# Grouped instance norm on one core: 64 KB rows in three 8 MB slots, and an earlier gamma

## The chip, the cores and the metric

The kernel runs on one core of a Trainium2 chip. The metric is the device time of one execution in microseconds, and the median of several runs is what is compared. The core has a tensor engine (PE), a vector engine (DVE), a scalar engine (ACT), a general engine (POOL) and a queue engine (SP), and 16 DMA engines that carry data between HBM, where input and output lie, and SBUF, the on-chip memory of 128 partitions. Transfers are issued here from SP's queue and from ACT's queue, and both run on the same 16 DMA engines.

## The reference

The input `x` has 4 x 128 = 512 channels of 256 x 256 float32 values, 134.2 MB. Each channel is normalised by its own mean and variance and multiplied by one gamma per channel of the group layout:

```
mu = x.mean(axis=(3, 4), keepdims=True)
var = ((x - mu) ** 2).mean(axis=(3, 4), keepdims=True)
out = (x - mu) / np.sqrt(var + 1e-5) * gamma[None, :, :, None, None]
```

Every value is read once from HBM and written once, 268.4 MB in all, if a channel stays in SBUF from its load to its store.

## The kernel before

A channel's 65536 values are cut into 8 rows of 8192 values (32 KB), one row to a partition, so a unit of 128 partitions holds 16 channels and 4 MB. There are 32 units (`U`) and six slots in SBUF (`xt0` to `xt5`, line 45).

The program writes its order out by hand (line 43 switches automatic scheduling off), so each engine executes its instructions in the order of the source. Lines 51 to 55 issue the first six loads: units 1 and 3 from ACT's queue, the others from SP's queue, and the row of 128 gammas (`g_row`) from SP's queue after unit 0. POOL then makes small constants: `eps_t`, `one`, and `navg` (lines 62 to 71), a 128 x 128 matrix with -1/65536 where two partitions hold the same channel, and zero elsewhere.

The loop over units (lines 100 to 133) does the following for each unit.

- DVE sums each row (line 102), and ACT squares each row and sums the squares (line 103). The squares themselves go into `junk` and aren't used.
- In unit 0 only, `gamma_columns` (lines 77 to 89) follows on DVE and PE: it repeats each gamma over the partitions of its channel and turns the row into columns `g_col` with eight small matmuls.
- PE multiplies both row sums by `navg` (line 113). This gives every partition minus the mean and minus the mean square of its channel.
- DVE combines the two to minus the variance (line 114), ACT takes the root (line 118), DVE the reciprocal (line 122) and the product with gamma (line 124).
- DVE rewrites the slot in place: (x - mean) x scale (line 127).
- ACT's queue issues the store (line 131), and SP's queue the load of the unit six later into the same slot (line 133). That load waits until the store has landed.

A float32 matmul appears in the profile as two passes, each a weight load (PEld) and a product (PE).

Of the kernel before, what the change touches and what calls it, by code (L numbers as in the profile page):

```python
# [1 line left out]

# [4 lines left out]

F32 = mybir.dt.float32
U8 = mybir.dt.uint8
ALU = mybir.AluOpType  # L10
ACTF = mybir.ActivationFunctionType
AX = mybir.AxisListType


@with_exitstack
def kernel(
    ctx: ExitStack,
    tc: tile.TileContext,
    x: bass.AP,
    gamma: bass.AP,  # L20
    out: bass.AP,
):
    nc = tc.nc
    B, G, C, H, W = x.shape
    P = nc.NUM_PARTITIONS
    HW = H * W
    n_ch = B * G * C
    S = 8
    K = P // S
    F = HW // S  # L30
    U = n_ch // K
    NG = (G * C) // K
    AHEAD = 6
    assert HW % S == 0 and (G * C) % K == 0

    xv = x.rearrange("b g c h w -> (b g c h w)").rearrange("(u p f) -> u p f", p=P, f=F)
    ov = out.rearrange("b g c h w -> (b g c h w)").rearrange("(u p f) -> u p f", p=P, f=F)
    gv = gamma.rearrange("g c -> (g c)")

    data = ctx.enter_context(tc.tile_pool(name="data", bufs=1))  # L40
    singles = ctx.enter_context(tc.tile_pool(name="singles", bufs=1))
    psum = ctx.enter_context(tc.tile_pool(name="psum", bufs=4, space=bass.MemoryType.PSUM))
    ctx.enter_context(tc.manual_schedule())

    slots = [data.tile([P, F], F32, name=f"xt{i}") for i in range(AHEAD)]

    def load(u, queue):
        queue.dma_start(out=slots[u % AHEAD][:], in_=xv[u])  # L48


    g_row = singles.tile([1, G * C], F32, name="g_row")
    for u in range(AHEAD):
        load(u, nc.scalar if u in (1, 3) else nc.sync)
        if u == 1:
            nc.sync.dma_start(out=g_row[:], in_=gv[None, :])


    eps_t = singles.tile([P, 1], F32, name="eps_t")
    nc.gpsimd.memset(eps_t[:], 1e-5)  # L59
    one = singles.tile([1, 1], F32, name="one")  # L60
    nc.gpsimd.memset(one[:], 1.0)
    navg = singles.tile([P, K, S], F32, name="navg")
    nc.gpsimd.memset(navg[:], -1.0 / HW)  # L63
    nc.gpsimd.affine_select(  # L64
        out=navg[:], in_=navg[:], pattern=[[-S, K], [0, S]], compare_op=ALU.is_ge,
        fill=0.0, base=0, channel_multiplier=1,
    )
    nc.gpsimd.affine_select(  # L68
        out=navg[:], in_=navg[:], pattern=[[S, K], [0, S]], compare_op=ALU.is_ge,
        fill=0.0, base=S - 1, channel_multiplier=-1,  # L70
    )
    navg_w = navg[:].rearrange("p k s -> p (k s)")
    g_rep = singles.tile([1, NG, K, S], F32, name="g_rep")
    g_ps = psum.tile([P, NG], F32, name="g_ps", bufs=1)
    g_col = singles.tile([P, NG], F32, name="g_col")

    def gamma_columns():
        nc.vector.tensor_copy(  # L78
            out=g_rep[:],
            in_=g_row[:].rearrange("o (n k) -> o n k", n=NG).unsqueeze(3).to_broadcast([1, NG, K, S]),  # L80
        )
        for n in range(NG):
            nc.tensor.matmul(  # L83
                out=g_ps[:, n : n + 1],
                lhsT=g_rep[:, n].rearrange("o k s -> o (k s)"),
                rhs=one[:],
                start=True, stop=True,
            )
        nc.vector.tensor_copy(out=g_col[:], in_=g_ps[:])  # L89

    junk = singles.tile([P, F], U8, name="junk")

    st = singles.tile([P, U, 2], F32, name="st")
    nvar = singles.tile([P, U], F32, name="nvar")
    std = singles.tile([P, U], F32, name="std")
    rstd = singles.tile([P, U], F32, name="rstd")
    scale = singles.tile([P, U], F32, name="scale")

    squares = []
    for u in range(U):  # L100
        t = slots[u % AHEAD]
        nc.vector.reduce_sum(out=st[:, u, 0:1], in_=t[:], axis=AX.X)  # L102
        square = nc.scalar.activation(  # L103
            out=junk[:], in_=t[:], func=ACTF.Square, accum_out=st[:, u, 1:2],
        )
        if u:

            tc.declare_no_dep(square.ins, squares[-1].ins, reason="junk, ordered by the root between")
        squares.append(square)
        if u == 0:  # L110
            gamma_columns()
        ps = psum.tile([P, 2], F32, name="ps")
        nc.tensor.matmul(out=ps[:], lhsT=navg_w, rhs=st[:, u], start=True, stop=True)  # L113
        nc.vector.tensor_scalar(  # L114
            out=nvar[:, u : u + 1], in0=ps[:, 0:1], scalar1=ps[:, 0:1],
            scalar2=ps[:, 1:2], op0=ALU.mult, op1=ALU.add,
        )
        nc.scalar.activation(  # L118
            out=std[:, u : u + 1], in_=nvar[:, u : u + 1], func=ACTF.Sqrt,
            bias=eps_t[:], scale=-1.0,  # L120
        )
        nc.vector.reciprocal(out=rstd[:, u : u + 1], in_=std[:, u : u + 1])  # L122
        g = u % NG
        nc.vector.tensor_mul(  # L124
            out=scale[:, u : u + 1], in0=rstd[:, u : u + 1], in1=g_col[:, g : g + 1],
        )
        nc.vector.tensor_scalar(  # L127
            out=t[:], in0=t[:], scalar1=ps[:, 0:1], scalar2=scale[:, u : u + 1],
            op0=ALU.add, op1=ALU.mult,
        )  # L130
        nc.scalar.dma_start(out=ov[u], in_=t[:])
        if u + AHEAD < U:
            load(u + AHEAD, nc.sync)


# [1 line left out]
_INS = ['x', 'gamma']  # L137
_OUTS = [((4, 8, 16, 256, 256), 'float32')]


# [23 lines left out]
```

## Time and profile before

| What | Value |
|---|---|
| median of 8 runs | 627.08 us (626.85 to 627.22) |
| the profiled execution | 626.85 us, of which its span, first to last instruction, is 625.1 us |
| DVE busy | 442.9 us, 71% of the span |
| ACT busy | 239.9 us, 38% |
| PE busy | 21.4 us, 3% |
| HBM | 134.22 MB read, 134.22 MB written, 429 GB/s over the span |
| line 102, DVE row sum, 128 x 8192 | 32 times 8683 ns |
| line 103, ACT squares, 128 x 8192 | 32 times 7030 ns, each followed by 186 ns to read the sum |
| line 127, DVE write-back, 128 x 8192 | 32 times 4550 ns |
| lines 114, 118, 122, 124 (128 x 1) | 287, 294, 164 and 159 ns |
| ACT's table load | two, 1283 ns each |
| loads | 32 of 4 MB, median 29.0 us from issue to landing (30 on SP's queue) |
| stores | 32 of 4 MB, median 64.1 us from issue to landing |

The table is read from the profile's summary page and its groups of instructions. A time between issue and landing includes the time that a transfer waits behind others on its queue. The share of busy time of an engine is a mean over the whole span.

### The profile page before, as it was taken

The numbers are of one execution on the slowest core, as the hardware profiler recorded it, in microseconds if no ns is written. First come the engines' busy times: TensorE is split into PE (matmuls) and PEld (weight loads), VectorE is DVE, ScalarE is ACT, GpSimd is POOL, SyncE is SP. The second block draws the span as 40 slices with busy tenths as digits, with TensorE's granted clock in tenths as the row PEclk, the third lists the DMA queues.
The fourth block names the chain that finished last, engine by engine and source line by source line (L and its number), as shares of the span: only waits on it lengthen the run. The fifth ranks groups of instructions, "written<-read, shape, count | busy, mean of one in ns | idle before, by whom it ended". The sixth has DMA issues, their size and how long they took to land.

```text
span 625.1 us, 628 instructions
## 1 busy us (share of the span) xinstructions
PE 21.4 (3%) x80; PEld 19.5 (3%) x80; DVE 442.9 (71%) x162; ACT 239.9 (38%) x98; POOL 1.3 (0%) x9
## 2 busy tenths in 40 slices
PE   0020000000000000000000000000000000000000
PEld 0020000000000000000000000000000000000000
DVE  0569999999898767867668676686766877667710
ACT  0435555544444423444224442244432444323400
POOL 0000000000000000000000000000000000000000
DMA  8999999999999999999999999999999999999998
GB/s 369 436 436 419 419 436 436 436 436 436 435 436 435 426 428 434 428 436 436 434 436 436 434 436 432 426 432 430 432 436 434 436 436 432 436 436 430 428 434 359
DMA packets 9220, 268.46 MB, mean 429 GB/s; under 512 B 1025, under 2 KB 1026, under 8 KB 1026
## 3 DMA queue, kind: packets, MB, share of 16 engines
q10 hardware_dynamic: 4896, 142.61, 52.8%
q1 hardware_dynamic: 4322, 125.83, 46.8%
q14 instruction: 2, 0.02, 0.0%
HBM read 134.22 MB, written 134.22 MB: 429 GB/s over the span
## 4 chain that ended last, share of the span: by engine, by line
DMA 62%; DVE 30%; PE 2%; issue 1%; ACT 1%; SPq 0%; ACTq 0%
DMA xt<-in_x_dram 55%; DVE st L102 24%; DMA out_dram<-xt 7%; DVE xt L127 5%; PE ps L113 2%; DVE nvar L114 1%; PE g_ps L83 1%; ACT std L118 0%; ACT L118 0%; DVE rstd L122 0%; DVE scale L124 0%; DVE g_rep L78 0%; SPq L48 0%; ACTq L118 0%
## 5 line engine op out<-in xcount | busy, mean ns | idle before, releaser
L102 DVE TENSOR_REDUCE st<-xt 128x1 f32<-128x8192 f32 x32 | 277.9, 8683 | 110.2 <-DMA xt<-in_x_dram 110.2
L103 ACT ACTIVATE junk<-xt 128x8192 uint8<-128x8192 f32 x32 | 224.9, 7030 | 266.1 <-DMA xt<-in_x_dram 212.1
L127 DVE TENSOR_SCALAR xt<-xt,ps,scale 128x8192 f32<-128x8192 f32 x32 | 145.6, 4550 | 1.2
L118 ACT ACTIVATE std<-nvar,eps_t 128x1 f32<-128x1 f32 x32 | 9.4, 294 | 76.0 <-DVE nvar L114 76.0
L113 PE MATMUL ps<-st,navg 128*128 128x2 f32 x64 | 17.9, 349 | 536.4 <-DVE st L102 536.4
L113 PEld LDWEIGHTS ps<-st,navg 128*128 128x128 f32 x64 | 16.1, 312 | 538.2 <-issue 538.2
L114 DVE TENSOR_SCALAR nvar<-ps 128x1 f32<-128x1 f32 x32 | 9.2, 287 | 23.5 <-PE ps L113 23.5
L122 DVE RECIPROCAL rstd<-std 128x1 f32<-128x1 f32 x32 | 5.2, 164 | 12.9 <-ACT std L118 12.9
L103 ACT ACTIVATION_READ_ACCUMULATOR junk<-xt 128x1 f32 x32 | 6.0, 186 | 0.0
L124 DVE TENSOR_TENSOR scale<-rstd,g_col 128x1 f32<-128x1 f32 x32 | 5.1, 159 | 1.1
L83 PE MATMUL g_ps<-one,g_rep 1*128 1x1 f32 x16 | 3.5, 347 | 32.1 <-DVE g_rep L78 32.1
L83 PEld LDWEIGHTS g_ps<-one,g_rep 1*128 1x128 f32 x16 | 3.5, 325 | 32.0 <-issue 32.0
L118 ACT ACT_TABLE_LOAD x1 | 1.3, 1283 | 6.8 <-DVE nvar L114 6.8
L89 DVE COPY g_col<-g_ps 128x8 f32<-128x8 f32 x1 | 0.2, 165 | 3.7 <-PE g_ps L83 3.7
L103 ACT ACT_TABLE_LOAD x1 | 1.3, 1283 | 1.7 <-PEq L148 1.7
L78 DVE COPY g_rep<-g_row 1x1024 f32<-1x1024 f32 x1 | 0.7, 672 | 0.0
L64 POOL TENSOR_SCALAR_AFFINE_SELECT navg<-navg 128x128 f32<-128x128 f32 x1 | 0.4, 403 | 0.1
L68 POOL TENSOR_SCALAR_AFFINE_SELECT navg<-navg 128x128 f32<-128x128 f32 x1 | 0.4, 398 | 0.1
L63 POOL MEMSET navg<- 128x128 f32 x1 | 0.2, 221 | 0.0
L148 POOL MEMSET const-bfloat16-1.0<- 128x1 bf16 x1 | 0.1, 101 | 0.0
L148 POOL MEMSET const-uint8-127<- 128x1 uint8 x1 | 0.1, 101 | 0.0
L59 POOL MEMSET eps_t<- 128x1 f32 x1 | 0.1, 99 | 0.3 <-POOLq L148 0.3
(3 smaller groups left out, 0.3 us busy)
## 6 DMA issues: line engine op xcount, KB each, us to landing
out_dram<-xt ACTq DMA_DIRECT2D x32, 4096.0 KB, 64.1
xt<-in_x_dram SPq DMA_DIRECT2D x30, 4096.0 KB, 29.0
xt<-in_x_dram ACTq DMA_DIRECT2D x2, 4096.0 KB, 31.5
g_row<-in_gamma_dram SPq DMA_DIRECT2D x1, 0.5 KB
```

Source lines behind the costliest of these rows:

```text
L64: nc.gpsimd.affine_select(out=navg[:], in_=navg[:], pattern=[[-S, K], [0, S]], compare_op=ALU.is_ge, fill=0.0, base=0, channel_multiplier=1,)
L68: nc.gpsimd.affine_select(out=navg[:], in_=navg[:], pattern=[[S, K], [0, S]], compare_op=ALU.is_ge, fill=0.0, base=S - 1, channel_multipli ...
L78: nc.vector.tensor_copy(out=g_rep[:], in_=g_row[:].rearrange("o (n k) -> o n k", n=NG).unsqueeze(3).to_broadcast([1, NG, K, S]),)
L83: nc.tensor.matmul(out=g_ps[:, n : n + 1], lhsT=g_rep[:, n].rearrange("o k s -> o (k s)"), rhs=one[:], start=True, stop=True,)
L102: nc.vector.reduce_sum(out=st[:, u, 0:1], in_=t[:], axis=AX.X)
L103: square = nc.scalar.activation(out=junk[:], in_=t[:], func=ACTF.Square, accum_out=st[:, u, 1:2],)
L113: nc.tensor.matmul(out=ps[:], lhsT=navg_w, rhs=st[:, u], start=True, stop=True)
L114: nc.vector.tensor_scalar(out=nvar[:, u : u + 1], in0=ps[:, 0:1], scalar1=ps[:, 0:1], scalar2=ps[:, 1:2], op0=ALU.mult, op1=ALU.add,)
L118: nc.scalar.activation(out=std[:, u : u + 1], in_=nvar[:, u : u + 1], func=ACTF.Sqrt, bias=eps_t[:], scale=-1.0,)
L122: nc.vector.reciprocal(out=rstd[:, u : u + 1], in_=std[:, u : u + 1])
L124: nc.vector.tensor_mul(out=scale[:, u : u + 1], in0=rstd[:, u : u + 1], in1=g_col[:, g : g + 1],)
L127: nc.vector.tensor_scalar(out=t[:], in0=t[:], scalar1=ps[:, 0:1], scalar2=scale[:, u : u + 1], op0=ALU.add, op1=ALU.mult,)
```

## The change

The unit becomes twice as large. A channel is now 4 rows of 16384 values (64 KB), and a unit holds 32 channels and 8 MB; there are 16 units (`V`) and three slots. Each load and each store of a unit is issued as two transfers of 64 rows, 4 MB each: the first 16 channels of the unit go to the even partitions (`t[0::2]`), the others to the odd partitions (`t[1::2]`). All loads are issued from SP's queue, and a half's next load waits for the same half's store. `navg` gets more steps on POOL, because partitions of one channel now lie two apart.

The gamma row is the first transfer on ACT's queue. A root of `eps_t` on ACT, whose result isn't used, comes before the loop and brings the table load with it, and the gamma columns are made ahead of the loop as well.

Within a unit, the squares are taken in two halves of 8192 columns, three matmuls replace one, and the write-back is split by columns: DVE takes the first 10240 (subtract and multiply) and ACT the other 6144 (multiply and add `shift`, which is minus mean times scale).

Unit 13, the third last, is stored in four transfers with rows of 32 KB. For the last unit the statistic is shared: DVE runs `bn_stats` over 18 pieces of 512 columns, ACT squares and sums the other 7168, and the two parts are added by matmuls that accumulate in one PSUM tile; its write-back and its store go in two halves of columns.

The core of the diff, without the unchanged small steps:

```diff
-    S = 8
-    F = HW // S
-    U = n_ch // K
-    AHEAD = 6
+    SL = 3
+    FW = HW // 4
+    FN = FW // 2
+    V = n_ch // 32
+    DV = 10240
+    BN, BW = 18, 512
...
+    xw = xf.rearrange("(v h r f) -> v h r f", h=2, r=P // 2, f=FW)
+    ow = of.rearrange("(v h r f) -> v h r f", h=2, r=P // 2, f=FW)
...
-    g_row = singles.tile([1, G * C], F32, name="g_row")
-    for u in range(AHEAD):
-        load(u, nc.scalar if u in (1, 3) else nc.sync)
-        if u == 1:
-            nc.sync.dma_start(out=g_row[:], in_=gv[None, :])
+    def load_slot(v):
+        t = slots[v % SL]
+        for h in range(2):
+            nc.sync.dma_start(out=t[h::2], in_=xw[v, h])
+
+    g_row = singles.tile([1, GC], F32, name="g_row")
+    nc.scalar.dma_start(out=g_row[:], in_=gv[None, :])
+    for v in range(SL):
+        load_slot(v)
...
+    root_eps = singles.tile([P, 1], F32, name="root_eps")
+    nc.scalar.activation(out=root_eps[:], in_=eps_t[:], func=ACTF.Sqrt)
...
+    for d in (-6, -4, -2, 0, 2, 4, 6):
+        nc.gpsimd.affine_select(
+            out=navg[:], in_=navg[:], pattern=[[-8, P // 8], [-1, 8]],
+            compare_op=ALU.not_equal, fill=-1.0 / HW, base=-d, channel_multiplier=1,
+        )
...
+    navg_b = singles.tile([P, P], F32, name="navg_b")
+    nc.gpsimd.tensor_scalar(
+        out=navg_b[:], in0=navg_w, scalar1=float(BN * BW), scalar2=None, op0=ALU.mult,
+    )
...
+    def sums(v, t, ps):
+        nc.vector.reduce_sum(out=st[:, v, 0:1], in_=t[:], axis=AX.X)
+        squared(v, t, 0, FN, 1)
+        squared(v, t, FN, FW, 2)
+        nc.tensor.matmul(out=ps[:, 0:1], lhsT=navg_w, rhs=st[:, v, 0:1], start=True, stop=True)
+        nc.tensor.matmul(out=ps[:, 1:2], lhsT=navg_w, rhs=st[:, v, 1:2], start=True, stop=False)
+        nc.tensor.matmul(out=ps[:, 1:2], lhsT=navg_w, rhs=st[:, v, 2:3], start=False, stop=True)
+
+    def sums_shared(v, t, ps):
+        e = BN * BW
+        bs = singles.tile([P, BN, nc.vector.BN_STATS_DIM], F32, name="bs")
+        for k in range(BN):
+            nc.vector.bn_stats(out=bs[:, k], in_=t[:, k * BW : (k + 1) * BW])
+        squared(v, t, e, FW, 1)
+        squared(v, t, e, FW, 0, ACTF.Identity)
+        mv = singles.tile([P, nc.vector.BN_AGGR_DIM], F32, name="mv")
+        nc.vector.bn_aggr(out=mv[:], in_=bs[:])
...
+        nc.tensor.matmul(out=ps[:], lhsT=navg_b[:], rhs=me[:], start=True, stop=False)
+        nc.tensor.matmul(out=ps[:], lhsT=navg_w, rhs=st[:, v, 0:2], start=False, stop=True)
...
-        nc.vector.tensor_scalar(
-            out=t[:], in0=t[:], scalar1=ps[:, 0:1], scalar2=scale[:, u : u + 1],
-            op0=ALU.add, op1=ALU.mult,
-        )
-        nc.scalar.dma_start(out=ov[u], in_=t[:])
-        if u + AHEAD < U:
-            load(u + AHEAD, nc.sync)
+        nc.vector.tensor_mul(out=shift, in0=ps[:, 0:1], in1=scale)
+
+        parts = [(0, FW)] if v < V - 1 else [(0, FN), (FN, FW)]
+        for a, b in parts:
+            m = a + DV * (b - a) // FW
+            nc.scalar.activation(
+                out=t[:, m:b], in_=t[:, m:b], func=ACTF.Identity, bias=shift, scale=scale,
+            )
+            nc.vector.tensor_scalar(
+                out=t[:, a:m], in0=t[:, a:m], scalar1=ps[:, 0:1], scalar2=scale,
+                op0=ALU.add, op1=ALU.mult,
+            )
+
+
+            for c, d in [(a, b)] if v != V - SL else [(0, FN), (FN, FW)]:
+                for h in range(2):
+                    nc.scalar.dma_start(out=ow[v, h, :, c:d], in_=t[h::2, c:d])
+        if v + SL < V:
+            load_slot(v + SL)
```

## The prediction

> **What bounds the kernel now.** I read the page's queue table and slices first, then the chain of waits, then stretches of the span, then the last microseconds in order of time. The page says who is full:
>
> ```profile
> GB/s 369 436 436 419 419 436 436 436 436 436 435 436 435 426 428 434 428 436 436 434 436 436 434 436 432 426 432 430 432 436 434 436 436 432 436 436 430 428 434 359
> DMA packets 9220, 268.46 MB, mean 429 GB/s; under 512 B 1025, under 2 KB 1026, under 8 KB 1026
> ...
> q10 hardware_dynamic: 4896, 142.61, 52.8%
> q1 hardware_dynamic: 4322, 125.83, 46.8%
> ...
> DMA xt<-in_x_dram 55%; DVE st L102 24%; DMA out_dram<-xt 7%; DVE xt L127 5%; PE ps L113 2%; DVE nvar L114 1%; PE g_ps L83 1%; ACT std L118 0%; ACT L118 0%; DVE rstd L122 0%; DVE scale L124 0%; DVE g_rep L78 0%; SPq L48 0%; ACTq L118 0%
> ```
>
> The two queues' packets fill 52.8 + 46.8 = 99.6% of 16 engines' span: no engine slot is left for a hidden gap. The chain's 24% of DVE comes from units 0 to 5, where the chain walks through compute although loads and stores go on beside it. The answer by stretches shows that (span, then busy times, last column GB/s):
>
> ```profile
> 22.00:46.00 24.00, 4.06 (x18) 3.99 (x18) 17.51 (x8) 11.18 (x5) 0.00 (x0) 1.00 0.99 427
> ...
> 66.00:120.00 54.00, 2.24 (x8) 2.01 (x8) 49.29 (x21) 24.38 (x11) 0.00 (x0) 1.00 1.01 437
> 120.00:580.00 460.00, 13.96 (x50) 12.54 (x50) 343.42 (x125) 183.59 (x75) 0.00 (x0) 1.00 1.00 433
> ...
> 596.00:622.00 26.00, 0.00 (x0) 0.00 (x0) 0.00 (x0) 0.00 (x0) 0.00 (x0) 1.00 1.02 440
> 622.00:623.70 1.70, 0.00 (x0) 0.00 (x0) 0.00 (x0) 0.00 (x0) 0.00 (x0) 1.00 0.14 58
> 623.70:625.10 1.40, 0.00 (x0) 0.00 (x0) 0.00 (x0) 0.00 (x0) 0.00 (x0) 1.00 0.00 0
> ```
>
> The rate stays within 1.5% of its mean from 22 to 622 us, whatever the engines do. The rest is 1.8 us before the first data packet and 1.4 us after the last. The end, in order of time:
>
> ```profile
> 561.09 7.03 ACT L103 ACTIVATE junk<-xt 128x8192 uint8<-128x8192 f32 x1 [9.30 <-DMA xt<-in_x_dram]
> ...
> 580.44 7.03 ACT L103 ACTIVATE junk<-xt 128x8192 uint8<-128x8192 f32 x1 [9.30 <-DMA xt<-in_x_dram]
> ...
> 590.91 4.55 DVE L127 TENSOR_SCALAR xt<-xt,ps,scale 128x8192 f32<-128x8192 f32 x1
> 595.49 0.34 ACTq L131 DMA_DIRECT2D out_dram<-xt  x1
> ```
>
> Two units land 580.44 - 561.09 = 19.35 us apart, the price of 8.39 MB (one load, one store): 433.5 GB/s. The last store is issued at 595.49 and needs 9.7 us alone, but lands at the end, 29.6 us later: about 20 us of older stores stand before it. So the tail's arithmetic is hidden too. Only three things can shorten this kernel: less time per byte in the stream, fewer extra events on the slowest DMA engine, or a shorter start or landing.
>
> **What the Trainium skill says.** "DMA: Bandwidth & Descriptors", section "Where 436 GB/s comes from", puts the ceiling at 16 ports x 32 B x 850 MHz = 435.2 GB/s; 8.39 MB would then take 19.275 us, and the trace's 19.35 us is 0.075 us above that. The same page, "Why small descriptors are slow (HBM only)", gives each packet a fixed overhead of about 3 cycles, 3.5 ns at that clock; 16 rows per engine in 19.35 us make 0.056 us of the 0.075, so trace and page agree roughly. In the trace's packet records a 32 KB row lasts 1213 ns, and the two queues alternate row by row. "SBUF — State Buffer", section "Door 1", says that partitions reach 16 DMA ports in groups of four, and those 32 apart share a port; the trace of before, with 128-partition transfers only, can't test that.
>
> **The change, part by part.**
>
> *64 KB rows.* Six 4 MB slots become three of 8 MB, 16 units of 32 channels, each moved as two 4 MB transfers of 64 rows (even, then odd partitions). Rows per engine fall from 512 to: loads 16 x 8 = 128; stores 14 x 8 + 2 x 16 = 144 (units 13 and 15 go out in 32 KB rows); 272 in all, 240 fewer. If all of the 0.075 us belongs to its 16 rows, a row costs 4.7 ns and the gain is 1.13 us; at the page's 3.5 ns it is 0.84 us. If a 64 KB row is carried as two it is nothing. I take 1.1. The number of transfers goes from 65 to 69: four more completion packets per engine, 9 ns each in the records, 0.04 us.
>
> *Gamma, its columns and Sqrt first.* In before the first unit's chain holds the row copy (0.67 us), the 16 gamma passes (3.54), the column copy (0.17) and a table load (1.28), some 6 us between 31 and 38 us. They move into the wait for unit 0, which ends at 22.6. Gamma (0.5 KB) heads ScalarE's queue, where nothing else stands, and SP's queue loses it (issue 0.32 us) from behind load 0. POOL gains seven selects of 0.40 us and one multiply, done long before 40 us. Worth nothing: during those 6 us the loads still run (to about 60 us), so DMA isn't waiting for the first store. Without this cover it would be 6 us.
>
> *Arithmetic per unit.* The sum over 16384 columns is twice 8.68 = 17.4 us on DVE; beside it two squares, 2 x (7.03 + 0.19) = 14.4 on ACT. Three matmuls instead of one make six passes: 0.57 + 4 x 0.22 (the gamma passes' pace) = 1.45. Then 0.29 + 0.29 + 0.16 + 2 x 0.16 plus gaps = 1.2. The write-back is split: DVE 10240 columns, 4.55 x 1.25 = 5.7, and ACT 6144, 7.03 x 0.75 = 5.3, beside it. Sum 17.4 + 0.15 + 1.45 + 1.2 + 5.7 = 25.9 us per 8 MB (before: 2 x 14.93 in the compute-paced start), against 2 x 19.35 = 38.7 us of DMA.
>
> *Is DMA ever starved by three slots?* Unit 0 lands at about 22.6 us (8 MB on one queue, as before 4 + 4 MB on two), is finished at 48.5, and its store enters the queue while loads last to 60 us alone; unit 1's store follows at 74.4. Store 0 and the rest of the loads fill the engines to 79, and half of load 3, released at about 70, carries on. Afterwards: when the first half of store v lands (T), the loads of v+3 take two half-rate turns, to T + 38.7; arithmetic ends at T + 64.6; the stores of v+1 and v+2 last until T + 96.7. So 32 us of cover per unit. The new waits on ScalarE's queue: store v+3 waits for semaphores of store v+1, which ends at T + 58, 7 us before v+3's arithmetic does; queued behind it are the next unit's squares, whose delay would eat into the 32 us only. SP's half-unit loads wait for the matching half store. Cost nothing.
>
> *The last units.* Storing unit 13 in 32 KB rows lets the 64 KB rows of load 15 take two thirds of each turn. Then at its landing some 14.5 us of unit 13 and 19.3 of unit 14 are still to store, 34 us. The last statistic takes 12.7 us on ACT (two passes over 7168 columns at 7.03/8192) or, on DVE, 18 bn_stats of 512: no row shows one; at the sum's pace 9.8 us, with 0.25 us overhead each 14.3; I take 11. With combination, chain and a half write-back the first half store comes 19 us after the landing, the second 22. Hidden by 12 us; even with equal shares of bytes 29 us would cover it.
>
> *End of the slowest engine.* In the packet records most engines end at 622.7 to 623.1 us, three later, the last at 623.65. Two instruction fetches of 8 KB (at 198 and 162 us) cost the engine that they hit 0.55 and 0.84 us. Whether the new program has them on a late engine isn't shown: between -0.6 and +0.3 us; I take -0.3.
>
> Sum: -1.1 + 0.04 - 0.3 = -1.4 us against the profiled execution's 626.85 (span 625.1, 1.75 around it): 625.45. The median of the runs shown is 0.23 above that execution, so 625.7; I say **625.6**.
>
> **Rivals.**
> *Rows of 64 KB bring nothing* (cut in two by the queue, or the 0.075 us belongs to the transfers' ends, whose number hardly changes): -0.3 or 0, 626.9. For it: the overhead is seen as one sum only. Against: a 512 B packet (27 ns) and a 32 KB one (1213) lie on a line with a fixed part.
> *Two engines on one port (slower).* Place: 64-partition strided transfers. Four rows to an engine in order would put engines with partitions 32 apart on the same ports at the same time. Price: loads alone run at half rate, unit 0 lands at 42 instead of 22.6 us, and until its store enters at about 68 us half the rate is lost: 34 us, so 660. It decides from the first 20 us. For it: the ports' map; against: the stride touches every port[...].
> *Restart of an empty queue (slower).* When the first store joined at 46 us, one round of load packets lasted 1.8 instead of 1.2 us. Each half load now waits for a half store, so SP's queue can run dry 26 times. At 0.6 us each: 15.6 - 1.4, so 641; at 0.1 us, 628.3. Against: ScalarE's first load packets, from an empty queue at 3.6 us, lasted 1.21 to 1.23.
>
> **How the numbers follow.** Forecast 0.66, 624.6 to 626.3; rows bring nothing 0.14; port 0.12; restart 0.08. A change counts from 0.2%, 1.25 us, about what the runs can tell from none, so faster means under 625.83: 0.45 of the forecast's 0.66 and 0.01 of the first rival. Slower: 0.12 + 0.07. The rest, 0.35, is no change. The range leaves out the port case, half of the restart case and thin tails: 624.5 to 628.6. The likeliest case's own range is 624.6 to 626.3.
>
> **What would show it.** Right: about 4,350 data rows instead of 8,192, a 64 KB row of about 2418 ns, units landing 38.65 us apart, DMA shares near 99.6%, and no idle DMA between 2 and 621 us. Wrong: a first landing well after 23 us, slices under 400 GB/s in the middle, a row longer than 2430 ns, or a last store issued later than 10 us before the end.

## The result: slower by half a per cent, and the profile after

| | median of the runs | lowest to highest | profiled execution | its span |
|---|---|---|---|---|
| before | 627.03 us (31 runs) | 626.8 to 627.5 | 626.85 | 625.1 |
| after | 630.53 us (11 runs) | 628.1 to 634.57 | 632.24 | 630.5 |

The ratio is 1.0061, with a 95% interval of 1.0049 to 1.0072: 3.5 us lost where 1.4 were forecast as a gain. The runs of the changed kernel also spread over 6.5 us, those of the kernel before over 0.7. A ratio leaves out runs over 1.5% above a kernel's fastest, although the clock is 1.0 in these too, and a median keeps them; where the two differ below (e6 and e18), the ratio is the lower estimate of the loss.

The page of the changed kernel, its rate in 40 slices and its queues (packets, MB, share of 16 engines' span):

```profile
GB/s 399 399 466 399 412 453 399 466 399 432 432 432 425 416 441 416 432 433 428 437 428 432 420 445 403 432 432 441 424 428 437 428 437 425 441 439 405 445 422 351
DMA packets 5445, 268.47 MB, mean 426 GB/s; under 512 B 1089, under 2 KB 1090, under 8 KB 1090
...
q1 hardware_dynamic: 2560, 134.22, 50.2%
q10 hardware_dynamic: 2882, 134.22, 49.2%
```

The rows are gone, as counted: 5445 packets less 1090 small ones are 4355, of which 4352 are data rows (128 for loads and 144 for stores on each engine), against 8192. The engines are as full as before, 99.4%, and still the same bytes take longer. So the time is in the packets themselves, not between them. The answer by stretches tells where (span, busy times, granted clock, DMA share, GB/s), first for the kernel before, then for the changed one:

```profile
60.00:120.00 60.00, 2.24 (x8) 2.01 (x8) 55.29 (x21) 29.95 (x13) 0.00 (x0) 1.00 1.01 436
120.00:500.00 380.00, 11.73 (x42) 10.54 (x42) 288.04 (x105) 153.92 (x63) 0.00 (x0) 1.00 1.00 433
500.00:560.00 60.00, 1.67 (x6) 1.50 (x6) 41.53 (x15) 22.25 (x9) 0.00 (x0) 1.00 1.00 433
```

```profile
22.00:46.00 24.00, 1.41 (x6) 1.36 (x6) 20.93 (x6) 17.39 (x6) 0.00 (x0) 1.00 1.01 437
60.00:120.00 60.00, 2.88 (x12) 2.71 (x12) 39.23 (x13) 33.90 (x11) 0.00 (x0) 1.00 0.98 419
120.00:500.00 380.00, 14.41 (x60) 13.55 (x60) 231.34 (x60) 196.66 (x60) 0.00 (x0) 1.00 1.00 430
500.00:560.00 60.00, 1.44 (x6) 1.35 (x6) 36.60 (x7) 32.65 (x9) 0.00 (x0) 1.00 0.99 427
```

This view books a row in the stretch in which it starts. A round of 64 KB rows is 2.4 us long, so a rate over 24 or 60 us can be some per cent off, as the shares of 1.01 and 0.98 say. If each row of the packet records is shared out by the time that it spends in a stretch, the rates are these:

| stretch, us | before, GB/s | after, GB/s |
|---|---|---|
| 22 to 46, loads alone | 432.6 | 433.9 |
| 46 to 60, the first stores join | 414.2 | 401.8 |
| 60 to 120 | 433.3 | 429.5 |
| 120 to 500 | 433.1 | 428.9 |
| 500 to 560 | 433.2 | 433.1 |

The loads alone are as fast as before, and so is the end. The loss lies between 46 and 500 us, where stores run beside the loads. A share of 1.00 at a lower rate means that packets last longer.

The trace's packet records say which. (They name no engine; where this document speaks of single engines, rows are strung together by one's end and the next one's start.) A 64 KB row alone lasts 2418 ns, as predicted. In this execution load rows (SP's queue) last 55 ns longer on average, 7.0 us per engine in all, and 18% of them by over 20 ns; store rows (ScalarE's queue) add 0.07 us. Of the 7.0 us, 4.5 lie between 120 and 500 us, 0.65 between 60 and 120, and 1.0 in the round in which the first stores join. In the kernel before the load rows' excess is 1.29 us per engine, about half of it in the round in which the first store joins. From 22 to 600 us the mean number of packets under way is 16.0, one for each engine. I call this excess the stretch of the loads.

Does the arithmetic or the end carry any of it? The start and the end of the changed kernel in order of time (start, duration, then engine, line, and in brackets the idle time before):

```profile
0.80 0.51 ACTq L58 DMA_DIRECT2D g_row<-in_gamma_dram  x1
...
23.04 17.22 DVE L123 TENSOR_REDUCE st<-xt 128x1 f32<-128x16384 f32 x1 [18.60 <-DMA xt<-in_x_dram]
...
48.69 1.17 ACTq L176 DMA_DIRECT2D out_dram<-xt  x2
```

```profile
578.56 10.78 DVE L134 BATCH_NORM_STATS2 bs<-xt 128x6 f32<-128x512 f32 x18 [6.17 <-DMA xt<-in_x_dram]
...
597.57 2.95 ACT L165 ACTIVATE xt<-xt,cf 128x3072 f32<-128x3072 f32 x1 [1.58 <-issue]
600.54 1.52 ACTq L176 DMA_DIRECT2D out_dram<-xt  x2
```

Unit 0 lands at 23.0 us (22.6 predicted) and its store is issued at 48.7 (48.5 predicted). The last store is issued at 600.54, 30 us before the end. Both ends of the program do what the prediction said; the middle doesn't.

### The profile page after: what moved, and what is told of

It is laid out like the page before. It is cut to its first block, busy times and chain, and to the rows that moved or that the text cites. A ratio compares the mean times of both kernels' runs of the same rounds, so it can differ in the third digit from the quotient of the medians.

```text
span 630.5 us, 667 instructions
## 1 busy us (share of the span) xinstructions
PE 24.5 (4%) x102; PEld 23.1 (4%) x102; DVE 371.7 (59%) x122; ACT 320.9 (51%) x99; POOL 4.7 (1%) x17
## 2 busy tenths in 40 slices
DMA packets 5445, 268.47 MB, mean 426 GB/s; under 512 B 1089, under 2 KB 1090, under 8 KB 1090
## 4 chain that ended last, share of the span: by engine, by line
DMA 59%; DVE 14%; another core or an unknown queue 12%; ACT 8%; PE 1%; issue 0%; SPq 0%; ACTq 0%; DVEq 0%
DMA out_dram<-xt 35%; DMA xt<-in_x_dram 24%; DVE st L123 14%; ACT xt L165 5%; ACT junk L114 2%; PE ps L126 0%; SPq L55 0%; PE ps L128 0%; PE ps L127 0%; ACTq L176 0%; ACT cf L157 0%; DVE cf L153 0%; DVE cf L158 0%; DVE cf L159 0%
## 5 line engine op out<-in xcount | busy, mean ns | idle before, releaser
L123 DVE TENSOR_REDUCE st<-xt 128x1 f32<-128x16384 f32 x15 | 258.3, 17219 | 185.9 <-DMA xt<-in_x_dram 185.9
L114 ACT ACTIVATE junk<-xt 128x8192 uint8<-128x8192 f32 (+1 forms) x32 | 223.2, 6976 | 196.2 <-DMA xt<-in_x_dram 193.0
L165 ACT ACTIVATE xt<-xt,cf 128x6144 f32<-128x6144 f32 (+1 forms) x17 | 88.5, 5207 | 12.4 <-DVE cf L160 10.8
L168 DVE TENSOR_SCALAR xt<-xt,ps,cf 128x10240 f32<-128x10240 f32 (+1 forms) x17 | 89.9, 5295 | 0.0
L157 ACT ACTIVATE cf<-cf,eps_t 128x1 f32<-128x1 f32 x16 | 4.7, 294 | 69.6 <-DVE cf L153 69.6
L126 PE MATMUL ps<-st,navg 128*128 128x1 f32 x30 | 8.8, 361 | 539.8 <-DVE st L123 539.8
L126 PEld LDWEIGHTS ps<-st,navg 128*128 128x128 f32 x30 | 7.5, 311 | 541.1 <-DVE st L123 504.8
L153 DVE TENSOR_SCALAR cf<-ps 128x1 f32<-128x1 f32 x16 | 4.6, 287 | 24.5 <-PE ps L128 23.1
L134 DVE BATCH_NORM_STATS2 bs<-xt 128x6 f32<-128x512 f32 x18 | 10.8, 677 | 6.2 <-DMA xt<-in_x_dram 6.2
L127 PE MATMUL ps<-st,navg 128*128 128x1 f32 x30 | 8.5, 352 | 0.0
L128 PE MATMUL ps<-st,navg 128*128 128x1 f32 x30 | 8.5, 352 | 0.0
L127 PEld LDWEIGHTS ps<-st,navg 128*128 128x128 f32 x30 | 8.2, 334 | 0.0
L128 PEld LDWEIGHTS ps<-st,navg 128*128 128x128 f32 x30 | 8.2, 333 | 0.0
L158 DVE RECIPROCAL cf<-cf 128x1 f32<-128x1 f32 x16 | 2.6, 164 | 5.8 <-ACT cf L157 5.8
```

The source lines that it names most:

```text
L114: sq = nc.scalar.activation(out=junk[:, : b - a], in_=t[:, a:b], func=func, accum_out=st[:, v, col : col + 1],)
L123: nc.vector.reduce_sum(out=st[:, v, 0:1], in_=t[:], axis=AX.X)
L126: nc.tensor.matmul(out=ps[:, 0:1], lhsT=navg_w, rhs=st[:, v, 0:1], start=True, stop=True)
L127: nc.tensor.matmul(out=ps[:, 1:2], lhsT=navg_w, rhs=st[:, v, 1:2], start=True, stop=False)
L128: nc.tensor.matmul(out=ps[:, 1:2], lhsT=navg_w, rhs=st[:, v, 2:3], start=False, stop=True)
L134: nc.vector.bn_stats(out=bs[:, k], in_=t[:, k * BW : (k + 1) * BW])
```

## The experiments

Times are medians, and kernels are named by the first part of their label; the kernel before, run beside each of them, took 627.0 to 627.1 us. "Stretch" is the excess of the load rows per engine in the one profiled execution, from the packet records; it is a mean over the engines, while the time follows the slowest one. Kernels in which an engine falls behind spread widely from run to run, so the ratios' intervals decide, not the one profile.

### Rows alone, with the structure kept

e1 puts a gap of 64 B between the halves of each slot's row, so that the same even and odd transfers go out as 32 KB rows; e2 has the same text without the gap, so 64 KB rows again. In both, VectorE's write-back is cut in two at the gap.

```
+    PAD = 16        # e1; 0 in e2
...
-    slots = [data.tile([P, FW], F32, name=f"xt{i}") for i in range(SL)]
+    slots = [data.tile([P, 2, FN + PAD], F32, name=f"xt{i}") for i in range(SL)]
...
-            nc.sync.dma_start(out=t[h::2], in_=xw[v, h])
+            nc.sync.dma_start(
+                out=t[h::2, :, :FN], in_=xw[v, h].rearrange("r (c f) -> r c f", c=2),
+            )
...
```

> The changed kernel, but each slot row has a gap of 64 bytes in its middle, so that every transfer of 64 partitions carries its rows as two pieces of 32 KB; same slots, same even and odd halves, same number of transfers. Row theory (a 64 KB load row stretches beside stores): 627.0, and no stretched loads. Split theory (even and odd partitions) and slot theory (three slots with half-unit hand-over): about 630.5, with stretched loads.

> The same text as e1_pad32 with a gap of 0 bytes: rows are 64 KB again. A control for the small edits of e1 (write-back in two DVE pieces). All theories: about 630.5, between 628.5 and 632.5.

Measured: e1 628.35 us, ratio 1.0028 (1.0015 to 1.0041); e2 632.87 us, 1.0089 (1.0069 to 1.011). With nothing changed but the length of a row, long rows cost 4.5 us by the medians and 3.8 by the ratios, where the prediction had them save 1.1. e1 itself stays 1.3 us above the kernel before, between the times of the two theories: its first packet starts at 2.23 us instead of 1.81, and two engines end 1.0 and 1.2 us later than the last one before. Its stretch is 1.45 us, about that of the kernel before. e2's stretch is 2.6 us on average and very uneven. In its profiled execution 15 engines end at 622.1 to 624.3 us, some of them earlier than any of before; but one, stretched by about 8 us, ends at 629.6. The last slice of its page shows that engine finishing alone:

```profile
GB/s 399 399 465 399 444 419 444 419 449 415 449 415 449 415 449 420 444 424 436 444 419 453 415 453 415 444 428 436 424 440 428 432 436 428 440 434 436 417 430 206
```

206 GB/s in the last 16 us, against 359 in the last slice of before: the bulk of the data is through, one engine isn't.

### The natural layout: loads and stores with rows of their own

These four keep three 8 MB slots and put 128 consecutive rows into 128 partitions, so that one transfer covers all partitions. e3 moves column halves both ways (32 KB rows), e4 whole units (64 KB), e5 loads whole and stores halves, e6 the reverse. `navg` and the gamma columns follow the layout, and a unit that moves in column halves moves as two transfers.

```
-    xw = xf.rearrange("(v h r f) -> v h r f", h=2, r=P // 2, f=FW)
+    xw = xf.rearrange("(v p f) -> v p f", p=P, f=FW)
...
-        for h in range(2):
-            nc.sync.dma_start(out=t[h::2], in_=xw[v, h])
+        for c, d in [(0, FW)]:        # [(0, FN), (FN, FW)] in e3 and e6
+            nc.sync.dma_start(out=t[:, c:d], in_=xw[v, :, c:d])
```

> The changed kernel with three 8 MB slots, but a unit's halves are column halves: two transfers of 128 partitions with 32 KB rows for each load and each store. Row theory and split theory: 627.0 (256 more 32 KB rows per engine pay back the 1.1 us). Slot theory: about 630.5.

> The changed kernel with three 8 MB slots and one transfer of 128 partitions with 64 KB rows for each load and each store, no even and odd halves. Row theory: about 630.5 with stretched loads. Split theory: about 626 without. Slot theory: 630.5 or more, since a load now waits for a whole store.

> Three 8 MB slots, transfers of 128 partitions: each load one transfer with 64 KB rows, each store two column halves with 32 KB rows. If the length of the load row is what stretches: 630, with loads above 2418 ns on some engines, like e4_full64. If the length of the store row before it is the cause: 627 to 628.5, no more stretch than e3_cols32.

> The same with the sizes exchanged: loads in two column halves with 32 KB rows, stores in one transfer with 64 KB rows. If the length of the load row is the cause: 627 to 628.5, and with the saved store rows (128 per engine fewer than before, 0.6 us) perhaps 626.5. If the store row is the cause: 630 with stretched loads.

| | loads | stores | median us | ratio (95%) | stretch us |
|---|---|---|---|---|---|
| e3 | 32 KB | 32 KB | 629.21 | 1.0044 (1.0032 to 1.0056) | 2.4 |
| e4 | 64 KB | 64 KB | 630.08 | 1.0057 (1.004 to 1.0073) | 2.9 |
| e5 | 64 KB | 32 KB | 627.94 | 1.0012 (1.0004 to 1.002) | 2.4 |
| e6 | 32 KB | 64 KB | 675.56 | 1.0664 (1.061 to 1.0718) | 8.2 |

e4 loses as much as the changed kernel without any even and odd halves, so these are not the cause as such. Seven of its 16 engines end at 622.1 to 622.3 us, where the first of before ended at 622.7: the saved rows are worth something. Three stretched by 4 to 6 us end at 624.4 to 626.7. e5 takes back the stores alone, their rows and their number of transfers, and gives 2.1 us back. e3 is not where either theory put it. With short rows both ways it still loses 2.2 us, more than e5 with its long load rows (the intervals are apart) and, within the spread, as much as e4. So in this layout long load rows beside short store rows cost nothing, and a loss of 2.2 us is there without any long row; why, these runs don't show. e6 was not foreseen. Its page and its waits, beside the changed kernel's wait for the same thing:

```profile
GB/s 374 437 422 383 399 381 397 393 368 431 450 399 420 397 418 447 408 407 433 289 399 451 416 414 431 429 300 400 431 422 424 435 460 323 400 418 412 260 128 370
...
q10 hardware_dynamic: 2594, 134.22, 47.6%
q1 hardware_dynamic: 4608, 134.22, 46.9%
```

```profile
DVE st L118 <- DMA xt<-in_x_dram: 230.0, 10, 40.3
```

```profile
DVE st L123 <- DMA xt<-in_x_dram: 185.9, 13, 18.6
```

The queues' shares add to 94.5%, so here engines do stand idle. The packet records show the two queues taking turns row by row whatever a row's length: 64 KB stores against 32 KB loads get two thirds of each engine's time while both are queued. The loads fall behind, engines drift apart, and VectorE waits up to 40.3 us for a unit. Store rows are stretched here too, by 13.5 us per engine. The profiled execution took 682.8 us, so the sizes are rough; the median is 48 us above before in any case.

### Single parts and the price of a row

e7 is the kernel before with gamma first on ScalarE's queue and the columns and the table made at once. e8 is the kernel before with its rows cut into 16 KB pieces by a gap, 512 more per engine. e11 is e5 with the ordinary statistic for the last unit.

```
+    nc.scalar.dma_start(out=g_row[:], in_=gv[None, :])      # e7
     for u in range(AHEAD):
         load(u, nc.scalar if u in (1, 3) else nc.sync)
-        if u == 1:
-            nc.sync.dma_start(out=g_row[:], in_=gv[None, :])
...
-    slots = [data.tile([P, F], F32, name=f"xt{i}") for i in range(AHEAD)]
+    slots = [data.tile([P, 2, F // 2 + 16], F32, name=f"xt{i}") for i in range(AHEAD)]      # e8
...
-        (sums if v < V - 1 else sums_shared)(v, t, ps)
+        sums(v, t, ps)      # e11
```

> The kernel before with the gamma part alone: gamma first on ScalarE's queue, its columns and the Sqrt table made while the first unit lands. The prediction's step (worth nothing, hidden behind loads): 627.0, within 0.4. If the first unit's chain counts: up to 6 us less.

> The kernel before with a gap of 64 bytes in the middle of each slot row, so that its 32 KB rows go as two pieces of 16 KB: 512 more pieces per engine. The prediction's price of 4.7 ns a row: plus 2.4 us, 629.4. With the 3.5 ns of the skill's page: plus 1.8, 628.8. If the 0.075 us per pair of transfers isn't the rows': 627.0.

> e5_load64_store32 with the ordinary statistic (one sum on VectorE, two squares on ScalarE) for the last unit as for all others. Step 'the last units are hidden behind the stores still queued': no change, 627.9 us within 0.5. Rival 'the last unit's arithmetic is on the path': the sum of 17.2 us takes the place of some 13 us of VectorE's part, so 631 to 632 us.

Measured: e7 626.97 us, ratio 1.0000 (0.9992 to 1.0007). e11 627.93 us, against 627.94 of e5. Neither part is worth anything, as predicted. e8 629.79 us, 2.78 above before. 2.78 us over 512 rows are 5.4 ns a row; its first packet starts 0.4 us later (2.20 for 1.81), and without that the price is 4.6 ns. The 4.7 of the prediction holds.

### One queue for both directions

If load rows stretch because other engines store at the same time, loads and stores in turns of 8 MB should not stretch. e9 (from e4) and e10 (from e3) send the stores out on SP's queue too, in a fixed order: store of unit v, then load of unit v+2, and at the end both last loads before the last three stores.

```
-                nc.scalar.dma_start(out=ow[v, :, c:d], in_=t[:, c:d])
-        if v + SL < V:
-            load_slot(v + SL)
+                nc.sync.dma_start(out=ow[v, :, c:d], in_=t[:, c:d])
+        if 0 < v < V - SL:
+            load_slot(v + SL - 1)
+        if v == V - SL - 1:
+            load_slot(V - 1)
```

> 64 KB rows both ways as in e4_full64, but every store goes out on the SP queue too, in an order written by hand (store of unit v, then load of unit v+2; at the end both last loads go ahead of the last three stores), so that loads and stores take turns of 8 MB instead of turns of one row, and an engine's loads stand beside other engines' stores only at the borders. Theory 'load rows stretch beside the stores of engines that are out of step': the stretch goes, all engines end together, about 622.2 us in the records as the undisturbed engines of e4, and the time is 625.0 to 626.2 us, below the kernel before and 4 to 5 us below e4. Rival 'a 64 KB row is slow by itself, or three slots starve the engines': the rows stay in one queue and the slots stay three, so 629.5 to 631 us as e4. A second rival, that one queue leaves gaps where it turns over (SP waits for the arithmetic of a unit, which leaves 5 to 10 us of queued work by my sums): 631 us or more, with DMA below 1.0 in the windows.

> The same single queue with the rows and column halves of e3_cols32 (32 KB rows both ways). If the theory of e9 holds, the difference between e9 and this one is the bare price of the rows, 256 rows per engine at 4.7 to 5.4 ns, so this one is 1.1 to 1.4 us above e9: 626.3 to 627.5 us, against 629.2 of e3 with its two queues. If the stretch comes from the length of a row and not from the queues, this one is below e9.

Measured: e9 630.86 us, 1.0058 (1.0046 to 1.0071); e10 631.47 us, 1.0073 (1.006 to 1.0085). The forecast of the time was wrong; the traces say why. No gap appears in e9:

```profile
46.00:60.00 14.00, 0.00 (x0) 0.00 (x0) 14.00 (x2) 13.97 (x4) 0.00 (x0) 1.00 1.08 435
60.00:120.00 60.00, 7.98 (x12) 7.81 (x12) 37.58 (x12) 30.72 (x10) 0.00 (x0) 1.00 0.99 419
120.00:500.00 380.00, 39.01 (x60) 38.17 (x60) 233.80 (x60) 199.02 (x60) 0.00 (x0) 1.00 1.00 433
```

The rate is down from 60 to 120 us, where the stream turns from loads to stores for the first times (422 GB/s, rows shared out as above). Row by row: a load row of e9 with no engine storing beside it is 3.5 ns too long (1177 rows between 60 and 560 us), one with any store beside it 80 ns (450 rows); in e10 1.1 and 51 ns. That looks as if other engines' stores held a load row up, but the order in time speaks against it. Of e9's 450 rows, the 280 or so that begin while a store is already under way are 10 ns too long. Most of the excess lies on the last rows of a block of loads, and at the first border these are late before any store begins: at 2418 ns all 16 would have ended by 60.96 us, the first store row on any engine begins at 61.26, and they are 0.6 to 1.3 us too long. They meet the stores because they are long. The kernels with two queues show the same where the first stores join. In the kernel before, all 16 load rows should have ended by 47.66 us, the first store row begins at 47.90, and they are 0.5 to 0.7 us too long; in the changed kernel the figures are 54.05, 54.59 and 0.8 to 1.3.

So at these places it is the turn from loads to stores that lengthens a load row, and not a store row under way; what an engine has in hand of its next store at that moment, the records don't show. A row inside a block of loads keeps its length. Some 3.3 us of stretch per engine gather at the borders (1.0 at the first one, at 58 us, and 450 x 80 ns / 16 = 2.3 after it), and I had counted these at nothing. e9 is 0.6 us below e10, where I expected 1.1 to 1.4; the intervals overlap.

### The cut of the transfers, or the layout

e5 pointed at the stores in the natural layout, their 64 KB rows or their single transfer. The same step in the changed kernel, e12, and three that change one thing each: e13 is e12 with loads as one transfer of 128 rows, e14 is e5 with loads cut into even and odd halves, e15 is the changed kernel with whole loads and its own half stores.

```
-    ow = of.rearrange("(v h r f) -> v h r f", h=2, r=P // 2, f=FW)
+    ow = of.rearrange("(v h r f) -> v r h f", h=2, r=P // 2, f=FW)      # e12, e13
...
-            for c, d in [(a, b)] if v != V - SL else [(0, FN), (FN, FW)]:
-                for h in range(2):
-                    nc.scalar.dma_start(out=ow[v, h, :, c:d], in_=t[h::2, c:d])
+            for c, d in [(a, b)] if b - a == FN else [(0, FN), (FN, FW)]:
+                nc.scalar.dma_start(out=ow[v, :, :, c:d], in_=t[:, c:d])
...
-        for h in range(2):
-            nc.sync.dma_start(out=t[h::2], in_=xw[v, h])
+        nc.sync.dma_start(out=t[:], in_=xw[v])      # e13, e15, with xw as v r h f
```

> The changed kernel itself, with nothing else altered, but each unit's store as two transfers of 128 rows of 32 KB (column halves) in place of two transfers of 64 rows of 64 KB; the loads keep their even and odd partitions and their rows of 64 KB. Theory 'the 64 KB rows of the stores are what stretches the loads' (from e4_full64 against e5_load64_store32, which had another layout): the loss goes down to that of e5 and the later first packet of this form, 0.3 us: 627.9 to 628.6 us, load rows longer by some 2.5 us per engine instead of 7.0. Rival 'the 64 KB rows of the loads, or the even and odd halves': no change, 630.0 to 631.0 us.

> e12_after_store32 with each unit's load as one transfer of 128 rows of 64 KB in place of two transfers of 64 rows (even, then odd partitions); the same addresses go to the same partitions, and the stores stay as two transfers of 32 KB rows. Now loads and stores are cut as in e5_load64_store32 and only the layout (which address lies in which partition) is that of the changed kernel. Theory 'the cut into even and odd halves leaves the load rows open to stretching': about 628 us, load rows longer by 2 to 3 us per engine. Rival 'the layout': 630 us and 5 us as in e12.

> The other way round: e5_load64_store32 with its natural layout, each load cut into two transfers of 64 rows, even and odd partitions. Theory 'the cut': about 630 us, load rows longer by 4 to 6 us per engine. Rival 'the layout': 628 us and 2.5 us.

> The changed kernel with its stores as they are (two transfers of 64 rows of 64 KB), and the loads as one transfer of 128 rows. If both the cut of the loads and the 64 KB rows of the stores cost, this one lies between e12 and e13 on one side and the changed kernel on the other: 629 to 630.5 us. If the stores' rows alone decide where the loads are whole, as e4_full64 against e5 says: 630 us; if the cut of the loads is all there is: 628 us.

| | layout | loads, 64 KB rows | stores | median us | ratio (95%) | stretch us |
|---|---|---|---|---|---|---|
| after | even/odd | 2 x 64 rows | 2 x 64 rows of 64 KB | 630.53 | 1.0061 (1.0049 to 1.0072) | 7.0 |
| e12 | even/odd | 2 x 64 rows | 2 x 128 rows of 32 KB | 630.19 | 1.0051 (1.0038 to 1.0065) | 5.0 |
| e13 | even/odd | 1 x 128 rows | 2 x 128 rows of 32 KB | 629.14 | 1.0029 (1.0018 to 1.0041) | 2.0 |
| e5 | natural | 1 x 128 rows | 2 x 128 rows of 32 KB | 627.94 | 1.0012 (1.0004 to 1.002) | 2.4 |
| e14 | natural | 2 x 64 rows | 2 x 128 rows of 32 KB | 629.39 | 1.0039 (1.0025 to 1.0052) | 3.2 |
| e15 | even/odd | 1 x 128 rows | 2 x 64 rows of 64 KB | 651.56 | 1.0392 (1.0376 to 1.0407) | 14.5 |

e12 went against my theory: in the changed kernel the stores alone give nothing back that can be told from the spread. The cut of the loads does count, by about 1.4 us in one layout (e12 and e13, whose intervals overlap a little) and 1.7 in the other (e14 and e5, apart), 0.3 of the latter being the later start. e15 fits none of the expectations. It has the bytes and the row lengths of the changed kernel, loses 24.5 us, and the engines are idle for only 1.3 us each between 22 and 600 us:

```profile
22.00:46.00 24.00, 1.41 (x6) 1.36 (x6) 20.78 (x6) 17.23 (x6) 0.00 (x0) 1.00 1.01 437
60.00:120.00 60.00, 2.88 (x12) 2.71 (x12) 35.57 (x12) 30.19 (x10) 0.00 (x0) 1.00 1.00 421
120.00:500.00 380.00, 12.97 (x54) 12.20 (x54) 218.95 (x55) 187.56 (x57) 0.00 (x0) 1.00 1.00 417
```

With loads alone the rate is that of the changed kernel (434 GB/s with the rows shared out), and then it is 417 at a full share. In the two units that I followed in its records (130 to 200 us) all engines are in step, and once in each unit all of them have a round in which a store row and the next load row together take 1.0 to 2.0 us more; in between, loads and stores alternate without loss.

### Addresses, or order

e16 is e15 with the two stores of a unit swapped, which changes only which addresses meet. e17 is the changed kernel with loads and stores swapped, e18 with the stores alone swapped, so that the even half of a slot is reloaded half a unit later.

```
-                for h in range(2):
+                for h in (1, 0):      # e16, e17, e18
                     nc.scalar.dma_start(out=ow[v, h, :, c:d], in_=t[h::2, c:d])
...
-        for h in range(2):
+        for h in (1, 0):      # e17
             nc.sync.dma_start(out=t[h::2], in_=xw[v, h])
```

> e15_load128_store64 with the two stores of each unit in the other order, odd partitions first. Loads wait for both stores of their slot in either case, so transfers, rows, queues and waits stay as they are; only which 4 MB of the output are written beside which rows of the input changes. Theory 'which addresses meet': the 24 us that e15 loses change by several us in one direction or the other. Rival 'the order of rows in the queues alone, whatever their addresses': 650 to 653 us again.

> The changed kernel with both the loads and the stores of each unit odd half first: every transfer meets the same partner as before the swap, and each slot half is reloaded after its own store as in the changed kernel. Both theories: 630.5 us within 0.7.

> The changed kernel with its stores odd half first and its loads as they are. The even half of a slot is now stored second, so its reload starts half a unit later and the loads run about four rows less ahead of the stores, as in e4_full64 (where load rows stood 14 to 15 rows ahead and were stretched by 2 to 10 ns, against 18 to 19 rows and 25 to 100 ns in the changed kernel). Theory 'the stretch depends on which load row stands beside which store row': the stretch per engine falls from 7.0 us to about 3 us, and the time to 628 to 629.5 us. Rival 'the row length of both directions alone': 630.5 us within 0.7. A third way: the later reload leaves the load queue short, and the time rises above 632 us with load-free stretches in the trace.

Measured: e16 652.69 us, 1.0412 (1.0396 to 1.0429), e15's loss again. So the pairing of addresses isn't what decides e15. e17 633.08 us, 629.0 to 637.5 from run to run, 1.0099 (1.0067 to 1.013): a miss by the median, though its interval and the changed kernel's just overlap. e18 644.02 us, 1.0193 (1.016 to 1.0226), with runs from 635.8 to 647.3: a miss; the later reload makes the loss larger, so my reading that a smaller lead of the loads over the stores calms the rows falls too. Only the third way that I had named, over 632 us, has the time right, and not its cause: the trace has one long stretch without loads (16.8 us, from 73 us), but e4 has one of 16.2 us and is 14 us faster, and the engines are idle for 0.6 us each. The packets are longer, by 8.6 us of load rows and 7.1 us of store rows per engine.

## Why the prediction was wrong

**The step that failed is the first, "64 KB rows": -1.13 us from 240 rows at 4.7 ns.** The count was right (4352 rows), the price of a row was right (e8: 4.6 to 5.4 ns) and so was the length of a long row by itself (2418 ns). The step took the time of a row as given, whatever turns between loads and stores it stands at. It isn't. In the profiled execution the sum runs: rows -1.1, first packet +0.3 (2.13 for 1.81 us), stretch of the loads +5.7 (7.0 less 1.3), together +4.9 of the 5.4 us by which that execution is longer. What the step left out is five times what it counted. e1 and e2 show it with nothing else changed: +3.8 to +4.5 us for long rows. Two of the signs of being wrong that the prediction names did appear: rows longer than 2430 ns, and slices under 400 GB/s. Only the first one counts, since six rounds of 64 KB rows that start in a slice of 15.8 us read 399 and seven read 466.

The stretch was in the profile before, in a small way: the prediction itself noted a round of 1.8 us packets when the first store joined, and used it only for the restart rival. It was the sign that a load row isn't always as long as its bytes make it. The prediction also read the rate as within 1.5% of its mean from 22 to 622 us; its own line of slices has 419 GB/s twice, 3% below, and the records give 414 from 46 to 60 us.

**"Is DMA ever starved by three slots?"** was right in its question: all 16 engines have work throughout, and the waits for slots cost no idle time. That it costs nothing was a little off. e1, with short rows and all else of the change, is 1.3 us above before, and e3, in the natural layout, 2.2; in e1 0.4 of this is the later first packet. A start later by 0.3 to 0.4 us was seen in every kernel whose even and odd partitions are loaded from different places or in different transfers, and in those with rows cut at a gap, and the sum had no term for it.

**"Gamma, its columns and Sqrt first"**: right, e7 at 1.0000. **"Arithmetic per unit"**: right, 23.0 to 48.5 us for unit 0 is 25.5 us against 25.9. **"The last units"**: right, bn_stats took 10.8 us where 11 was taken, the last store had 30 us of cover, and e11 shows the shared statistic worth nothing. **"End of the slowest engine"**, -0.3, has the wrong sign: engines end at 627.3 to 628.9 us. The last one does so because of its rows (stretch 8.2 us), the next, at 628.8, in part because of an instruction fetch of 0.9 us at 530 us, the kind of event that the term had in view.

**The rivals.** "Rows bring nothing" had the right doubt and no room for a loss. "Two engines on one port" is out: 434 GB/s with loads alone, first landing at 23.0. The case rested on the Trainium skill's "SBUF — State Buffer", section "Door 1", which puts partitions 32 apart on one port; these even and odd transfers lose nothing by it, and which partitions an engine moves at a time isn't in the records. "Restart of an empty queue" comes nearest in size (0.1 us each gave 628.3) but names another mechanism: apart from the start and the first store round, the last row of a half load was the most stretched in the changed kernel, 77 to 97 ns on average, the first 39 to 48, and no engine stopped. The range, 624.5 to 628.6, ended 1.9 us below the result because no rival had long packets at full occupancy.

**What stays open.** Shown: load rows with no store under way keep their length once the stream runs (2418 ns and 0.6 ns more on average in the changed kernel from 22 to 46 us, 3.5 more in e9), and the last ones before a turn to stores don't (e9, and the first stores of the kernel before and of the changed one). In the mixed stream from 60 to 560 us the 32 KB load rows of the kernel before and of e1 stand beside stores all through and are 0.1 and 0.3 ns too long on average, the 64 KB ones 51 ns in the changed kernel and 9 in e2: long rows make it worse where the structure is kept (e1, e2). The stores (e4, e5) and the cut of the loads (e13, e14) each carry part of it; how transfers are cut and chained matters more than either (e15, e16, e18). Not shown is what in the memory or the DMA engines makes a load row wait, nor why e3 loses 2.2 us with short rows. That e16 keeps e15's loss speaks against particular addresses meeting. Nor can I say from these runs which combination will be calm before running it: the times that I expected of e1, e3, e6, e9, e10, e12, e15, e17 and e18 failed. No version here beats the kernel before.

## What to carry to other kernels

When a stream already fills the DMA engines, fewer and longer rows can save only the price of the rows (here 1.1 us of 627), while longer rows where loads and stores alternate can cost several times that; so time an edit to rows on the chip before building on it. Read the packets' durations, not only the engines' share: full occupancy at a lower rate means longer packets, and a rate over a short stretch needs a look at how rows at its edges are counted. If loads and stores share the engines through two queues, don't give the stores the longer rows (675 us), and look at the spread of the runs, which rose together with the loss here (6.5 us against 0.7).

## What the runs showed of the hardware that I had not expected

- The last load row before a turn to stores lasts longer before any store row has begun: by 0.5 to 0.7 us on all 16 engines in the kernel before, 0.8 to 1.3 in the changed one, 0.6 to 1.3 in e9.
- Two queues on one engine took turns row by row, not byte by byte, as the prediction had it for unit 13. That 64 KB stores beside 32 KB loads then take two thirds of the time and make 675.6 us of 627 (e6) was not expected.
- The same bytes in the same 64 KB rows took from 630.1 us (e4) to 652.7 us (e16), with the engines full up to the last few microseconds, by the cut and the order of the transfers alone.
- Only the load rows were stretched in the changed kernel (7.0 us per engine, stores 0.07); store rows as well in e6 (64 KB rows: 13.5), e15 (4.2), e16 (3.9) and e18 (6.3).
- Even and odd transfers of 64 partitions ran at 434 GB/s with loads alone, as the kernel before did (433), but kernels with them sent their first packet 0.3 to 0.4 us later.
